# MLP down projection in a post-normalised decoder layer: seven 2x2-block products in two sweeps in place of eight blocks

## The chip, the cores and the metric

The kernel runs on one core of a Trainium2 chip. The metric is device time in microseconds (us) of one execution, lower is better.

## What is computed

One layer of a hybrid decoder: 512 tokens, width 1024, hidden width 4096, float32. Three sub-layers (a token mixer, cross-attention into 256 memory tokens, an MLP), each followed by `h = LayerNorm(ALPHA * h + f(h))`. The change concerns the third:

```
def sq_relu_mlp(h, w_up, b_up, w_down, b_down):
    u = jax.nn.relu(h @ w_up + b_up)
    return (u * u) @ w_down + b_down        # (512, 4096) @ (4096, 1024)

h = layer_norm(ALPHA * h + sq_relu_mlp(...), ln_ffn_g, ln_ffn_b)
```

## The kernel before

Every large product is done in three terms. An operand is split into a high part, the value cast to float32r, and a low part, the rest (`split`: a cast, then a subtraction); `mm3` adds high x high, high x low and low x high in PSUM. A matmul takes a 128 x 128 stationary tile and up to 512 moving columns.

The kernel's operations are recorded first and then put in order by a planner (`Program.issue`), which keeps a model of the engines, gives every operation a time, and issues in that order; operations recorded by `either` (as `any_tt`) go to the engine that the model finds free first. After that each engine's order is fixed, SyncE's list of DMAs too. All instructions are issued from line 355 of the kernel before, so the profile tells them apart by tile names. Tiles come from pools that are reused in turn: 4 buffers for raw weights (`wr`), 5 each for high and low parts of weights (`wh`, `wl`), 31 pages of 4 KB per partition, 8 PSUM banks.

The MLP works on blocks of 128 hidden units, 32 of them. `up(f)` loads a column block of `w_up` (`r_up`, 512 KB), splits it (`h_up`, `l_up`), runs 24 matmuls into a bank (`ps_up`), then relu on ScalarE (`ur`), the square on VectorE, and the split of the result into a page `u`. It does 16 blocks, then their part of the down projection: for each half of the 1024 columns, 4 banks (one for each block of 128 tokens, `ps_dn`) take 16 hidden blocks; VectorE adds them to the residual `res`. Then 16 more blocks, and the second part of the down projection in `gemm_tok`: eight banks (4 token blocks x 2 halves), the last four hidden blocks done token block by token block (`tail`), so that the norm of one token block (`after_ffn`) runs beside the matmuls of the next. For the last token block the second half goes in two quarters (`ps_dn2e`). The weights are `r_dn`, `h_dn`, `l_dn`. In the norm of the first three token blocks ScalarE scales and GpSimd adds the shift; the last is done on VectorE, and stored in halves.

Of the kernel before, what the change touches and what calls it, by code (L numbers as in the profile page):

```python
# [141 lines left out]
class Program:  # L142
# [97 lines left out]
    def issue(self, look):  # L240
# [28 lines left out]
        dma = 0.0  # L269
        holding, done = set(), [False] * len(ops)  # L270
        front = 0
        order = []

        def slots(op, at):

# [83 lines left out]
def f32(ap):  # L359
    return ap.bitcast(F32)  # L360
# [3 lines left out]
def trunk_kernel(ctx: ExitStack, tc: tile.TileContext, x, mem, ln_in_g, ln_in_b, w_in, gate_w2,  # L364
# [728 lines left out]

    def residual(res, t, parts, name):

        n = 512 if len(parts) == 2 else 256
        st = small.tile([128, D // n, 6], F32, "st_" + name)
        for cc, o in parts:
            nc.vector.tensor_tensor(res[t][:, cc], o, res[t][:, cc], op=OP.add)
            for c0 in range(cc.start, cc.stop, n):  # L1100
                nc.vector.bn_stats(st[:, c0 // n, :], res[t][:, c0:c0 + n])
        return mean_scale(st, name)
# [85 lines left out]
        gain_shift(res, gb, t, GAIN_LATER)  # L1188


    NF = DFF // 128 // 2
    slack[0] = M_SLACK

    def up(f, split):
# [4 lines left out]
        nc.scalar.activation(r, ps, AF.Relu, bias=bup[:, f:f + 1])  # L1199
        u = page([2, T], F32R, "u2")  # L1200
        nc.vector.tensor_tensor(r, r, r, op=OP.mult)
        nc.scalar.copy(u[:, 0, :], r)
        nc.vector.tensor_tensor(u[:, 1, :], r, f32(u[:, 0, :]), op=OP.subtract)
        return u

    us = [up(f, f < 4) for f in range(NF)]
    for c in range(2):
        banks = [bank("ps_dn") for _ in range(NT)]
        cc = slice(512 * c, 512 * c + 512)
        for f in range(0, NF, 2):  # L1210
            wh, wl = load_rows(w_down, 128 * f, "dn", 2, 512 * c, 512)
            for k in range(2):
                for t in range(NT):
                    tt = slice(128 * t, 128 * t + 128)
                    u = us[f + k]
                    mm3(banks[t], u[:, 0, tt], u[:, 1, tt], wh[:, k, :], wl[:, k, :], f + k == 0, f + k == NF - 1)
        for t in range(NT):
            nc.vector.tensor_tensor(res[t][:, cc], banks[t], res[t][:, cc], op=OP.add)
    us = [up(NF + f, False) for f in range(NF)]
    gbf = gb_rows(ln_ffn_g, ln_ffn_b, 1.0, "ffn")  # L1220

    def after_ffn(t, parts):
        y = res[t]
        mv, rs = residual(res, t, parts, "ffn")
        if t < NT - 1:
            nc.vector.scalar_tensor_tensor(y, y, mv[:, 0:1], gbf[0], op0=OP.subtract, op1=OP.mult)
            nc.scalar.activation(y, y, AF.Copy, scale=rs)
            pool_tt(y, y, gbf[1], OP.add)
            nc.sync.dma_start(out[128 * t:128 * t + 128, :], y)
            return  # L1230
        for cc in (slice(0, 512), slice(512, D)):
            nc.vector.scalar_tensor_tensor(y[:, cc], y[:, cc], mv[:, 0:1], gbf[0][:, cc], op0=OP.subtract, op1=OP.mult)
        for cc in (slice(0, 512), slice(512, D)):
# [43 lines left out]
```

## Time and profile before

| what | us |
|---|---|
| median of 3 runs (lowest, highest) | 845.61 (843.9, 846.23) |
| profiled execution, device time | 845.03 |
| profiled execution, first to last instruction (span) | 843.3 |
| TensorE busy | 815.2 |
| VectorE busy | 535.7 |
| ScalarE busy | 281.8 |
| GpSimd busy | 167.1 |

Busy times of different engines overlap. PE is TensorE's matmuls and PEld its weight loads, which run beside them; DVE is VectorE, ACT ScalarE, POOL GpSimd, SP SyncE, which issues the DMAs. The granted clock is a share of 2.4 GHz. All rows are of one profiled execution.

### The profile page before, as it was taken

What the parts mean: (1) busy time and instruction counts of PE and PEld (TensorE: products, weight loads), DVE (VectorE), ACT (ScalarE), POOL (GpSimd) and SP (SyncE); (2) the same over time, 40 slices, a digit from 0 to 9 for tenths busy, and PEclk for the clock granted to TensorE, in tenths of its full rate; (3) what the DMA queues carried; (4) which work ended last, traced back from release to release, by engine and by line L of the source; (5) the groups of instructions that cost most, each with busy time, mean ns of one, the idle gap of its engine ahead of it and who ended that gap; (6) DMA issues with size and microseconds to landing.
All of it is one profiled execution on the core that took longest, in us unless ns stands there. A gap on an engine that the chain in (4) does not pass through costs nothing.

```text
span 843.3 us, 11052 instructions
## 1 busy us (share of the span) xinstructions
PE 815.2 (97%) x4270; PEld 682.8 (81%) x4270; DVE 535.7 (64%) x936; ACT 281.8 (33%) x566; POOL 167.1 (20%) x179
## 2 busy tenths in 40 slices
PE   6999999999999899989999999999999999999996
PEld 4998768778777888888788898888888888888885
DVE  7657999997449984896544885444343444443337
ACT  4316633577445440334330344442000244430001
POOL 5300241465622210244420300000000000000005
PEclk8999999999999999999999999999999999999998
DMA  8440331603245444033313034333243333232102
GB/s 192 106 123 13 100 89 26 175 8 100 75 165 175 136 132 143 1 101 101 124 51 100 2 100 135 93 97 117 89 145 99 96 89 96 94 121 87 67 1 99
DMA packets 104660, 81.50 MB, mean 97 GB/s; under 512 B 21792, under 2 KB 90400, under 8 KB 104608
## 3 DMA queue, kind: packets, MB, share of 16 engines
q1 hardware_dynamic: 101296, 73.81, 29.6%
q10 hardware_dynamic: 3312, 7.00, 2.4%
q8 instruction: 33, 0.54, 0.3%
q14 instruction: 19, 0.16, 0.1%
HBM read 77.91 MB, written 2.10 MB: 95 GB/s over the span
## 4 chain that ended last, share of the span: by engine, by line
PE 75%; DVE 19%; issue 3%; ACT 1%; DMA 1%; POOL 1%; DVEq 0%; ACTq 0%; POOLq 0%
PE ps_up L355 21%; PE ps_dn L355 20%; PE ps_wmo L355 4%; PE ps_wo L355 4%; PE ps_q L355 3%; DVE acc L355 3%; PE ps_gv_iw L355 2%; PE ps_iq L355 2%; PE ps_km L355 2%; PE ps_z L355 2%; DVE res L355 2%; DVE m L355 2%; PE ps_vm L355 1%; PE ps_dq L355 1%; PE ps_mo L355 1%
## 5 line engine op out<-in xcount | busy, mean ns | idle before, releaser
L355 PE MATMUL ps_up<-h2T,h_up 128*128 128x512 f32 (+1 forms) x576 | 162.6, 368 | 0.0
L355 PE MATMUL ps_dn<-h_dn,u 128*128 128x512 f32 x504 | 155.4, 389 | 0.0
L355 PEld LDWEIGHTS ps_up<-h2T,h_up 128*128 128x128 f32 x576 | 105.2, 191 | 17.7 <-DVE h2T L355 0.2
L355 PEld LDWEIGHTS ps_dn<-h_dn,u 128*128 128x128 f32 x504 | 94.6, 188 | 19.6
L355 PE MATMUL ps_up<-h2T,l_up 128*128 128x512 f32 (+1 forms) x288 | 105.5, 368 | 0.5 <-DVE ve_mem L355 0.5
L355 PE MATMUL ps_dn<-l_dn,u 128*128 128x512 f32 x252 | 98.0, 389 | 0.0
L355 POOL TENSOR_TENSOR rs_ffn<-ve_ffn,mhalf 128x1 f32<-128x1 f32 x4 | 5.6, 1389 | 326.4 <-DVE ve_ffn L355 326.4
L355 PEld LDWEIGHTS ps_up<-h2T,l_up 128*128 128x128 f32 x288 | 54.8, 191 | 9.5 <-DVE l_up L355 0.7
L355 DVE TENSOR_SCALAR h_dn<-r_dn 128x1024 fp32r<-128x1024 f32 x21 | 14.6, 694 | 68.2 <-PE ps_dn L355 68.2
L355 DVE TENSOR_TENSOR ur<-ur 128x512 f32<-128x512 f32 x32 | 22.0, 691 | 55.0 <-ACT ur L355 55.0
L355 PEld LDWEIGHTS ps_dn<-l_dn,u 128*128 128x128 f32 x252 | 47.3, 188 | 9.9
L355 ACT ACTIVATE ur<-ps_up,bup 128x512 f32<-128x512 f32 x32 | 22.1, 690 | 73.0 <-PE ps_up L355 73.0
L355 PE MATMUL ps_q<-h1T,h_wmq 128*128 128x256 f32 (+1 forms) x192 | 45.2, 326 | 0.0
L355 ACT CAST h_up<-r_up 128x1024 fp32r<-128x1024 f32 x27 | 28.0, 1047 | 45.3 <-PE ps_dn L355 42.4
L355 DVE TENSOR_TENSOR l_up<-r_up,h_up 128x1024 fp32r<-128x1024 f32 x32 | 39.0, 1223 | 5.5 <-ACT h_up L355 5.3
L355 DVE TENSOR_TENSOR l_dn<-r_dn,h_dn 128x1024 fp32r<-128x1024 f32 x32 | 39.2, 1226 | 3.8 <-ACT h_dn L355 3.0
L355 PE MATMUL ps_wmo<-h_wmo,oT 128*128 128x512 f32 x128 | 40.7, 393 | 0.0
L355 PE MATMUL ps_wo<-h_wo,mix 128*128 128x512 f32 x128 | 40.3, 392 | 0.0
L355 DVE TENSOR_TENSOR u<-ur,u 128x512 fp32r<-128x512 f32 x32 | 22.1, 692 | 19.9 <-ACT u L355 19.9
L355 PEld LDWEIGHTS ps_q<-h1T,h_wmq 128*128 128x128 f32 x192 | 32.6, 195 | 2.5 <-DVE h1T L355 0.2
L355 PE MATMUL ps_q<-h1T,l_wmq 128*128 128x256 f32 (+1 forms) x96 | 31.1, 328 | 0.0
L355 ACT ACTIVATE res<-res,rs_ffn 128x1024 f32<-128x1024 f32 x3 | 3.5, 1152 | 79.8 <-POOL rs_ffn L355 79.8
(371 smaller groups left out, 1787.8 us busy)
## 6 DMA issues: line engine op xcount, KB each, us to landing
r_up<-in_w_up_dram SPq DMA_DIRECT2D x32, 512.0 KB, 3.8
r_dn<-in_w_down_dram SPq DMA_DIRECT2D x32, 512.0 KB, 3.7
r_kvv<-in_w_mem_kv_dram SPq DMA_DIRECT2D x8, 512.0 KB, 3.9
r_kvk<-in_w_mem_kv_dram SPq DMA_DIRECT2D x8, 512.0 KB, 4.0
r_wo<-in_w_out_dram SPq DMA_DIRECT2D x8, 512.0 KB, 4.7
r_wmq<-in_w_mem_q_dram SPq DMA_DIRECT2D x8, 512.0 KB, 4.2
r_wmo<-in_w_mem_o_dram SPq DMA_DIRECT2D x8, 512.0 KB, 3.3
x<-in_x_dram SPq DMA_DIRECT2D x8, 256.0 KB, 4.3
```

The source lines that it names most:

```text
L355: f(*[real(a) for a in args], **{k: real(a) for k, a in kwargs.items()})
```

## The change

The 2x2-block product of the squared activations by `w_down` (two token halves x two hidden blocks, by two hidden blocks x two column halves) is done with seven block products instead of eight (Strassen's algorithm, in Winograd's form). Two neighbouring hidden blocks make a pair, 16 pairs. The seven products are accumulated over all pairs, and only at the end put together. There are not enough banks for all of them, so there are two sweeps.

In the first sweep each pair runs its two up blocks and, behind those of the next pair, the products 1, 6 and 4, for two token blocks each (six banks beside the two of `ps_up`). The squared activations stay in a page `keep`; their sums and differences (`s2`, and others in place) are made on it, and operands are split as `ends` and `mid`. Of the weights, `r_dn0` and `r_dn1` are loaded, four differences are made (`t3`, and three in place), two of these are stored in a DRAM scratch (`t13`, one for each pair, two DMAs of 256 KB), and two groups are split (`h_dn512`, `h_dn1024`). Between the sweeps the six banks are worked into the residual. In the second sweep each pair splits its `keep` page (`a0`, `a1`), loads the scratch and the second weight block (512 KB each), splits both, and runs the products 7, 5, 3 and 2 in eight banks. The last `TAIL` = 4 pairs are split into pages (`b0`, `b1`) and run product by product, with the norms between them; all of the norm is now on VectorE. The square of `up` may go to VectorE or ScalarE; here it is always ScalarE, and it writes the page without a split.

```diff
-    us = [up(f, f < 4) for f in range(NF)]
-    for c in range(2):
-        banks = [bank("ps_dn") for _ in range(NT)]
...
-    gemm_tok(us, w_down, NF, NF, "dn2", after_ffn, ends=res[NT - 1])
+    def first_weights(i):
+        r0, r1 = raw_down(i, 0), raw_down(i, 1)
+        t3 = temp("t3")
+        any_tt(t3, r1[:, R], r0[:, R], OP.subtract)
+        any_tt(r0[:, R], r0[:, R], r0[:, L], OP.subtract)
+        kept = dram.tile([128, 1024], F32, f"t13_{i}")
+        nc.sync.dma_start(kept[:, L], r0[:, R])
+        nc.sync.dma_start(kept[:, R], t3)
+        sums.append(kept)
+        any_tt(r1[:, R], r1[:, R], r0[:, R], OP.subtract)
+        any_tt(r1[:, L], r1[:, R], r1[:, L], OP.subtract)
...
+        split_weights(r0[:, L], hi[0], lo[0])
+        split_weights(r1, hi[1], lo[1])
...
+    def first_products(i):
+        pg = keep[i]
+        block = lambda n: pg[:, n, :]
+        ends = page([2, 2, 256], F32R, "ends")
+        two_parts(ends[:, 0], ends[:, 1], pg[:, 0:4:3, :])
+        any_tt(block(0), block(0), block(1), OP.subtract)
+        any_tt(block(1), block(1), block(3), OP.add)
+        s2 = temp("s2", 256)
+        any_tt(s2, block(3), block(0), OP.subtract)
+        mid = temp("mid", 512, F32R).reshape(2, 256)
+        two_parts(mid[:, 0], mid[:, 1], s2)
+        any_tt(block(3), block(2), s2, OP.subtract)
+        b11, t2, t4 = first_weights(i)
...
+    for p in range(2):
+        six = temp("six")
+        nc.scalar.copy(six, banks["6", p])
+        add(p + 2, L, banks["4", p], OP.subtract)
+        add(p, L, banks["1", p])
+        nc.vector.tensor_tensor(six, banks["1", p], six, op=OP.add)
+        later.append(six)
...
+            for t, cc in ((p, R), (p + 2, L), (p + 2, R)):
+                any_tt(res[t][:, cc], res[t][:, cc], later[p], OP.add)
...
+    for p in range(2):
+        for n, name in enumerate(("7", "5", "3", "2")):
+            for i, todo in enumerate(rest):
+                products(banks, [todo[n]], p, False, i == TAIL - 1)
+            if name == "7":
+                add(p + 2, L, banks[name, p])
+                add(p + 2, R, banks[name, p])
+            elif name == "5":
+                add(p + 2, R, banks[name, p])
+                add(p, R, banks[name, p])
+                after_ffn(p + 2)
+            elif name == "3":
+                add(p, R, banks[name, p])
+            else:
+                add(p, L, banks[name, p])
+                after_ffn(p)
```

How the orders move is shown at three places. The first is SyncE's list of DMAs in the first sweep. Before, in the second group of up blocks and into the down projection, it holds loads only (a name in brackets is the engine or DMA queue whose semaphore the DMA waits for):

```order
L355 DMA r_up<-in_w_up_dram 128x8x128 [waits DMAHW2_49,DVE_49]
L355 DMA r_up<-in_w_up_dram 128x8x128 [waits DMAHW3_49,DVE_49]
L355 DMA r_up<-in_w_up_dram 128x8x128 [waits DMAHW4_49,DVE_49]
L355 DMA r_up<-in_w_up_dram 128x8x128 [waits DMAHW5_49,DVE_49]
L355 DMA r_up<-in_w_up_dram 128x8x128 [waits DMAHW6_49,DVE_49]
L355 DMA r_dn<-in_w_down_dram 128x2x512 [waits DMAHW7_49,DVE_49]
```

Now a round of the first sweep holds the two loads of `w_down`, the two stores into the scratch (`t_5`), each behind VectorE, and then the loads of the next up blocks:

```order
L356 DMA r_dn_5659<-in_w_down_dram 128x1024 [waits DMAHW2_49,DVE_49]
L356 DMA r_dn_5661<-in_w_down_dram 128x1024 [waits DMAHW0_49,DVE_49]
L356 DMA t_5_5666<-t_5663 128x512 [waits DVE_49]
L356 DMA t_5_5666<-r_dn_5659 128x512 [waits DMAHW5_49,DVE_49]
L356 DMA r_up<-in_w_up_dram 128x8x128 [waits DMAHW3_49,DMAHW1_49,Activation_49]
L356 DMA r_up<-in_w_up_dram 128x8x128 [waits DMAHW4_49]
```

The stores stand ahead of the loads of `w_up`, and SyncE takes its list in order.

The second place is TensorE where the last up block ends. Before, the down matmuls of that half follow at once, on pages made long before:

```order
L355 MATMUL ps_up<-h2T_4804,h_up 128x512 x2
L355 MATMUL ps_up<-h2T_4804,l_up 128x512
L355 MATMUL ps_dn_6695<-h_dn_6567,u_6152 128x512
L355 MATMUL ps_dn_6695<-l_dn_6573,u_6152 128x512
L355 MATMUL ps_dn_6695<-h_dn_6567,u_6152 128x512
L355 MATMUL ps_dn_6701<-h_dn_6567,u_6152 128x512
```

Now, behind the last up block and the first fifteen product matmuls of pair 14, TensorE has the last three of pair 14 (bank 5208 is product 4, second token block), three of product 7 of the second sweep (bank 6894), and pair 15, whose operands come from that last up block (5171 and 5196 are product 1, 5188 is product 4):

```order
L356 MATMUL ps_dn_5208<-h_dn_6751,ends 128x512
L356 MATMUL ps_dn_5208<-l_dn_6757,ends 128x512
L356 MATMUL ps_dn_5208<-h_dn_6751,ends 128x512
L356 MATMUL ps_dn_6894<-h_dn,a_6271 128x512
L356 MATMUL ps_dn_6894<-l_dn,a_6271 128x512
L356 MATMUL ps_dn_6894<-h_dn,a_6805 128x512
L356 MATMUL ps_dn_5171<-h_dn_6764,ends 128x512
L356 MATMUL ps_dn_5171<-l_dn_6769,ends 128x512
L356 MATMUL ps_dn_5188<-h_dn_6813,ends 128x512
L356 MATMUL ps_dn_5188<-l_dn_6815,ends 128x512
L356 MATMUL ps_dn_5196<-h_dn_6764,ends 128x512
L356 MATMUL ps_dn_5196<-l_dn_6769,ends 128x512
```

Of pair 15 the matmuls on the high part of `ends` come first, and the first matmuls of the second sweep have moved in between.

The third place is VectorE's end. Before, its last rows are the last token block (`res_2606`) alone, in two quarters at the end:

```order
L355 TENSOR_TENSOR res_2606<-ps_dn_6731,res_2606 128x512 [waits PE_49]
L355 BN_STATS st_ffn<-res_2606 128x6 [waits DVE_49]
L355 BN_STATS st_ffn<-res_2606 128x6
L355 TENSOR_TENSOR res_2606<-ps_dn2e,res_2606 128x256 [waits PE_49]
L355 BN_STATS st_ffn<-res_2606 128x6 [waits DVE_49]
L355 TENSOR_TENSOR res_2606<-ps_dn2e,res_2606 128x256 [waits PE_49]
L355 BN_STATS st_ffn<-res_2606 128x6 [waits DVE_49]
L355 BN_AGGR mv_ffn<-st_ffn 128x2 [waits DVE_49]
L355 TENSOR_SCALAR ve_ffn<-mv_ffn 128x1 [waits DVE_49]
L355 SCALAR_TENSOR_TENSOR res_2606<-res_2606,mv_ffn,gbc_ffn 128x512 x2
L355 SCALAR_TENSOR_TENSOR res_2606<-res_2606,rs_ffn,bbc_ffn 128x512 [waits DVE_49,Pool_49]
L355 SCALAR_TENSOR_TENSOR res_2606<-res_2606,rs_ffn,bbc_ffn 128x512 [waits DVE_49]
```

Now there are two token blocks in work at the end (`res_2608` and `res_2596`), in halves of 512, and the last sums from PSUM (bank 6982 is product 2) stand between the steps of the other block's norm:

```order
L356 TENSOR_SCALAR ve_ffn<-mv_ffn 128x1 [waits DVE_49]
L356 SCALAR_TENSOR_TENSOR res_2608<-res_2608,mv_ffn,gbc_ffn 128x512
L356 TENSOR_TENSOR res_2596<-res_2596,ps_dn_6982 128x512 [waits PE_49]
L356 SCALAR_TENSOR_TENSOR res_2608<-res_2608,mv_ffn,gbc_ffn 128x512
L356 SCALAR_TENSOR_TENSOR res_2608<-res_2608,rs_ffn,bbc_ffn 128x512 [waits DVE_49,Pool_49]
L356 SCALAR_TENSOR_TENSOR res_2608<-res_2608,rs_ffn,bbc_ffn 128x512 [waits DVE_49]
L356 BN_STATS st_ffn<-res_2596 128x6
L356 BN_AGGR mv_ffn<-st_ffn 128x2 [waits DVE_49]
L356 TENSOR_SCALAR ve_ffn<-mv_ffn 128x1 [waits DVE_49]
L356 SCALAR_TENSOR_TENSOR res_2596<-res_2596,mv_ffn,gbc_ffn 128x512 x2
L356 SCALAR_TENSOR_TENSOR res_2596<-res_2596,rs_ffn,bbc_ffn 128x512 [waits DVE_49,Pool_49]
L356 SCALAR_TENSOR_TENSOR res_2596<-res_2596,rs_ffn,bbc_ffn 128x512 [waits DVE_49]
```

Eight of these twelve are 512-wide steps, and the rows ahead of them are of the same kind.

## Rows read from the trace of the kernel before

**Rows 1.** The page, part 1: engine, busy us, share of the span, instructions.
```profile
PE 815.2 (97%) x4270; PEld 682.8 (81%) x4270; DVE 535.7 (64%) x936; ACT 281.8 (33%) x566; POOL 167.1 (20%) x179
```

**Rows 2.** The chain that ended last: start us, us, engine, work, count.
```profile
309.89 32.67 PE ps_wo L355 x144
...
493.99 80.91 PE ps_up L355 x416
574.89 87.04 PE ps_dn L355 x384
661.93 87.04 PE ps_up L355 x384
748.98 84.32 PE ps_dn L355 x372
833.29 2.88 PE ps_dn2e L355 x24
...
838.82 0.74 DVE res L355
839.56 0.66 DVEq L1273
```

**Rows 3.** Windows: us, length, busy of PE, PEld, DVE, ACT, POOL, clock, DMA, GB/s.
```profile
309.00:343.00 34.00, 34.00 (x157) 28.27 (x156) 17.78 (x22) 4.49 (x5) 0.56 (x1) 1.00 0.46 140
486.80:490.40 3.60, 3.59 (x17) 3.59 (x18) 3.60 (x5) 0.00 (x0) 1.47 (x1) 0.54 0.56 165
490.40:493.90 3.50, 3.50 (x30) 3.34 (x29) 1.26 (x4) 1.31 (x3) 0.00 (x0) 0.99 0.93 274
574.90:661.90 87.00, 87.00 (x385) 72.03 (x385) 35.42 (x39) 3.31 (x4) 0.00 (x0) 1.00 0.37 115
661.90:748.90 87.00, 87.00 (x386) 72.03 (x385) 41.15 (x48) 35.01 (x46) 0.00 (x0) 1.00 0.30 91
748.90:833.10 84.20, 84.20 (x373) 69.73 (x372) 36.67 (x47) 4.56 (x5) 8.39 (x5) 1.00 0.19 63
836.20:843.30 7.10, 0.00 (x0) 0.00 (x0) 3.92 (x8) 0.00 (x0) 2.45 (x2) 0.67 0.37 148
```

**Rows 4.** Groups by shape on VectorE: count, busy us, mean ns, idle before.
```profile
L355 DVE TENSOR_TENSOR l_dn<-r_dn,h_dn 128x1024 fp32r<-128x1024 f32 x32 | 39.2, 1226 | 3.8 <-ACT h_dn L355 3.0
...
L355 DVE TENSOR_TENSOR u<-ur,u 128x512 fp32r<-128x512 f32 x32 | 22.1, 692 | 19.9 <-ACT u L355 19.9
...
L355 DVE TENSOR_SCALAR h_dn<-r_dn 128x1024 fp32r<-128x1024 f32 x21 | 14.6, 694 | 68.2 <-PE ps_dn L355 68.2
...
L355 DVE TENSOR_TENSOR res<-ps_dn,res 128x512 f32<-128x512 f32 x16 | 11.0, 690 | 11.8 <-PE ps_dn L355 11.8
...
L355 DVE TENSOR_TENSOR mpT<-ps_mpt,mpT 128x256 fp32r<-128x256 f32 x16 | 6.1, 421 | 1.0 <-ACT mpT L355 0.9
...
L355 DVE BATCH_NORM_STATS2 st_ffn<-res 128x6 f32<-128x512 f32 x6 | 4.2, 695 | 0.2
...
L355 DVE TENSOR_SCALAR sp<-sa 128x512 fp32r<-128x512 f32 x6 | 2.5, 422 | 0.0
...
L355 DVE SCALAR_TENSOR_TENSOR res<-res,mv_ffn,gbc_ffn 128x512 f32<-128x512 f32 x2 | 1.4, 744 | 0.0
```

**Rows 5.** Groups by shape on ScalarE.
```profile
L355 ACT CAST h_up<-r_up 128x1024 fp32r<-128x1024 f32 x27 | 28.0, 1047 | 45.3 <-PE ps_dn L355 42.4 <-PE ps_wmo L355 2.9
L355 ACT ACTIVATE ur<-ps_up,bup 128x512 f32<-128x512 f32 x32 | 22.1, 690 | 73.0 <-PE ps_up L355 73.0
L355 ACT CAST u<-ur 128x512 fp32r<-128x512 f32 x32 | 19.8, 620 | 23.3 <-DVE ur L355 23.3
```

**Rows 6.** Groups by shape on GpSimd.
```profile
L355 POOL TENSOR_TENSOR res<-res,bbc_ffn 128x1024 f32<-128x1024 f32 x3 | 7.2, 2384 | 3.8 <-ACT res L355 3.8
```

**Rows 7.** The page, part 6: DMA issues, count, size, median us to landing.
```profile
r_dn<-in_w_down_dram SPq DMA_DIRECT2D x32, 512.0 KB, 3.7
```

More of the change, by code (lines that the diff above doesn't have):

```diff
@@ L246, in issue @@
                 ops[j].after.append(i)
+        self.order = order = []
         line = sorted(range(len(ops)), key=lambda i: ops[i].prio)
@@ L271, in issue @@
         front = 0
-        order = []
         def slots(op, at):
@@ L376, in pool @@
         got = ctx.enter_context(tc.tile_pool(name=name, bufs=bufs or 1, **kw))
-        return VPool(got, tag, bufs, space is not None)
+        return VPool(got, tag, bufs, space is PSUM)
     cst = pool("cst", None, 0)
@@ L1188, in trunk_kernel, with up @@
         gain_shift(res, gb, t, GAIN_LATER)
-    NF = DFF // 128 // 2
+    NP = DFF // 256
     slack[0] = M_SLACK
-    def up(f, split):
+    def up(f, split, to):
         wh, wl = load_cols(w_up, [(128 * f, 128, 0)], "up")
@@ L1219, in trunk_kernel @@
-    us = [up(NF + f, False) for f in range(NF)]
-    gbf = gb_rows(ln_ffn_g, ln_ffn_b, 1.0, "ffn")
-    def after_ffn(t, parts):
-        y = res[t]
[L1224 to L1231, printed above, removed]
+        b = bup[:, f:f + 1]
@@ new lines, in trunk_kernel, with products @@
+    sums = []
+    L, R = slice(0, 512), slice(512, 1024)
+    def products(banks, todo, p, start, stop):
+        tt = slice(128 * p, 128 * p + 128)
+        for name, (ah, al), (bh, bl) in todo:
+            mm3(banks[name, p], ah[:, tt], al[:, tt], bh, bl, start, stop)
+    def first_weights(i):
[9 more added lines that the diff above has]
+        any_tt(r1[:, L], r1[:, R], r1[:, L], OP.subtract)
+        hi = [wh_pool.tile([128, n], F32R, f"h_dn{n}") for n in (512, 1024)]
+        lo = [wl_pool.tile([128, n], F32R, f"l_dn{n}") for n in (512, 1024)]
+        split_weights(r0[:, L], hi[0], lo[0])
+        split_weights(r1, hi[1], lo[1])
+        return [(hi[0], lo[0]), (hi[1][:, R], lo[1][:, R]), (hi[1][:, L], lo[1][:, L])]
@@ new lines, in trunk_kernel @@
+    banks = {}
+    keep = []
+    def first_products(i):
[11 more added lines that the diff above has]
+        b11, t2, t4 = first_weights(i)
+        if i == 0:
+            for name in ("1", "6", "4"):
+                for p in range(2):
+                    banks[name, p] = bank(f"ps_dn{name}")
+        for p in range(2):
+            products(banks, [("1", (ends[:, 0, 0, :], ends[:, 1, 0, :]), b11), ("6", (mid[:, 0], mid[:, 1]), t2),
+                             ("4", (ends[:, 0, 1, :], ends[:, 1, 1, :]), t4)], p, i == 0, i == NP - 1)
@@ new lines, in add @@
+    def add(t, cc, o, op=OP.add):
+        nc.vector.tensor_tensor(res[t][:, cc], res[t][:, cc], o, op=op)
+    for i in range(NP):
+        pg = page([4, 256], F32, "keep")
+        keep.append(pg)
+        for e in range(2):
+            up(2 * i + e, i < 2, pg.reshape(1024)[:, 512 * e:512 * e + 512])
+        if i:
+            first_products(i - 1)
+    first_products(NP - 1)
+    later = []
+    for p in range(2):
+        six = temp("six")
[4 more added lines that the diff above has]
+        later.append(six)
@@ new lines, in trunk_kernel, with second_parts @@
+    nc.clock += DOWN_LATER
+    for p in range(2):
+        for t, cc in ((p, R), (p + 2, L), (p + 2, R)):
+            any_tt(res[t][:, cc], res[t][:, cc], later[p], OP.add)
+    nc.clock -= DOWN_LATER
+    gbf = gb_rows(ln_ffn_g, ln_ffn_b, 1.0, "ffn")
+    def second_parts(i, tail):
+        a = [page([4, 256], F32R, f"a{n}") for n in range(2)]
+        two_parts(a[0], a[1], keep[i])
+        r0 = wr_pool.tile([128, 1024], F32, "r_t13")
+        nc.sync.dma_start(r0, sums[i])
+        r1 = raw_down(i, 1)
+        right = []
+        for r in (r0, r1):
+            if tail:
+                hi, lo = (page([1024], F32R, f"b{n}") for n in range(2))
+            else:
+                hi, lo = wh_pool.tile([128, 1024], F32R, "h_dn"), wl_pool.tile([128, 1024], F32R, "l_dn")
+            two_parts(hi, lo, r)
+            right += [(hi[:, L], lo[:, L]), (hi[:, R], lo[:, R])]
+        left = [(a[0][:, n, :], a[1][:, n, :]) for n in range(4)]
+        return [("7", left[0], right[1]), ("5", left[1], right[0]), ("3", left[3], right[3]), ("2", left[2], right[2])]
@@ new lines, in trunk_kernel, with after_ffn @@
+    for i in range(NP - TAIL):
+        todo = second_parts(i, False)
+        if i == 0:
+            for name, *_ in todo:
+                for p in range(2):
+                    banks[name, p] = bank(f"ps_dn{name}")
+        for one in todo:
+            for p in range(2):
+                products(banks, [one], p, i == 0, False)
+    rest = [second_parts(i, True) for i in range(NP - TAIL, NP)]
+    def after_ffn(t):
+        y = res[t]
+        st = small.tile([128, 2, 6], F32, "st_ffn")
+        for c, cc in ((1, R), (0, L)):
+            nc.vector.bn_stats(st[:, c, :], y[:, cc])
+        mv, rs = mean_scale(st, "ffn")
+        for cc in (L, R):
```

33 lines of the change are left out of this document (16 added, 17 removed).

## The prediction

> **What bounds the kernel now.** The chain of waits comes first, read at its end [rows 2]: from 493.99 us to 836.17 us it holds nothing but TensorE, the up and down matmuls of the MLP one after the other, and only then VectorE for the last layer norm. The reader should see that no wait stands between the stretches: 384 down matmuls take 87.04 us, 384 up matmuls 87.04 us, which is 226.7 ns for each 512-column matmul whatever the tile. The windows say the same of the other engines [rows 3]: over 574.9 to 833.1 TensorE is busy all the time at granted clock 1.00 (2.4 GHz), VectorE 35 to 41 us of each stretch of 84 to 87, ScalarE 3 to 35, the DMA engines a share of 0.19 to 0.37. TensorE is busy 97% of the whole span [rows 1]. So in the MLP a matmul taken away is worth its 226.7 ns, as long as the engines with room left can do what replaces it. Ahead of the MLP the rows of every engine's order are the same in both kernels, so nothing moves before the first up blocks.
>
> **What it removes.** The down projection has 32 hidden blocks x 4 token blocks x 2 halves x 3 terms = 768 matmuls of 512 columns (384, 372, and 24 of half width in the last 2.88 us [rows 2]). Now it has 16 pairs x 7 products x 2 token blocks x 3 = 672, of the same shape. 96 x 0.2267 = 21.76 us; the 24 half matmuls took 2.88 us where twelve whole ones take 2.72, so 0.16 more. **Term 1: -21.92 us.** That the price stays 226.7 ns when accumulators change every three matmuls can be read: the mixer's output projection cycles eight banks like that, 144 matmuls in 32.67 us, 226.9 ns [rows 2], clock 1.00 [rows 3].
>
> **First sweep.** A pair is now 48 up matmuls and 18 products (1, 6, 4), 66 x 0.2267 = 14.96 us of TensorE. VectorE's share of a pair, counted in its order and priced by [rows 4]: three 1024-wide differences (3.68), two 1024-wide casts (1.39), one 512-wide cast (0.42), six 512-wide differences (4.15), five 256-wide sums (2.09): 11.7 us, 78%. ScalarE: one 1024-wide cast, two relus, two squares and two casts priced as the 512-wide one [rows 5]: 1.05 + 1.38 + 4 x 0.62 = 4.9 us. GpSimd has nothing. So no engine passes TensorE, if the in-order queues don't lock into each other. Two places were followed. The weight pools (5 buffers, filled in the order in which TensorE uses them) let the split of a block begin when the block five before it is used up, 9 us or more before TensorE wants it. And SyncE: the two stores of a pair wait for VectorE, and the next pair's two w_up loads stand behind them. The stores go out after VectorE's second instruction of the pair; load (3.7 us [rows 7]), cast and split (2.3 us) make 6 us from there, and TensorE wants the first of these blocks some 20 us after the stores. At the start, pair 0's products are wanted at 509.6 us (416 matmuls of the first stretch, of which the last twelve up blocks take 65.3 us, end at 574.9); VectorE, which has residual work left from the layer norm in both kernels, ends their splits at about the same time. **Term 2: 0**, and the cover is VectorE's 3.2 free us per pair; without it each us too long counts 14 times.
>
> **The joint of the sweeps.** Let T be the end of the last up matmul. TensorE's order puts 18 products of pair 14 and three of product 7 behind it, 21 matmuls, 4.76 us. In that time the last block goes through ScalarE: relu 0.69, a cast, square 0.62, two 1024-wide casts 2.1, cast 0.62, which gives pair 15's left operand at about T + 4.5 and its low part from VectorE at T + 6.1 (two 1024-wide differences stand ahead of it). TensorE does the six high matmuls first, until T + 6.1. Then the second sweep wants eight banks where the first holds six: product 5 may start when VectorE has subtracted product 4 from the residual, 3 when ScalarE has copied product 6, 2 when VectorE has added product 1 into it. Followed with [rows 4, 5] the last bank is free at about T + 12.9, and the 60th matmul behind T ends at T + 13.8 instead of 60 x 0.2267 = 13.6; the two 256-wide steps given to GpSimd (a quarter of its 2.38 us row [rows 6], 0.6 each) are the closest. I take **1 us for term 3**; below 0, above 4.7, the whole cover of 21 matmuls lost.
>
> **Second sweep.** A pair is 24 matmuls, 5.44 us. VectorE: three 1024-wide differences, 3.68 us; ScalarE three casts, 3.14 us [rows 4, 5]. VectorE comes late into it: behind the bank work it reaches the split of the third pair's first tile at T + 17 and ends it at T + 18.2, wanted at T + 19.7. From there it gains 1.8 us a pair. SyncE's loads are now two tiles of 512 KB per pair, 1.05 MB in 5.44 us = 193 GB/s. Over a whole stretch the trace has 115 GB/s at DMA share 0.37, and for 3.5 us 274 GB/s at 0.93 [rows 3]: 193 would be a share of 0.62 to 0.66. The last four pairs are held in pages so that TensorE can finish one accumulator after another; that wants the t13 tile of pair 15 about 14 us before its turn. By the load time of [rows 7] and four load buffers it is split some 2.6 us early. **Term 4: 0**, above 3.
>
> **The tail.** Let E be the end of the last matmul. Before, VectorE's last instruction ended at 840.22, 4.05 us after 836.17 [rows 2]. Now product 2 of token block 0 ends at E - 10.88 and VectorE reaches its addition at E - 10.5, with 7 additions from PSUM (4.83), 6 statistics (4.17) and 12 scale-and-shift steps (8.93) to do [rows 4], and six small ones that I put at 0.4 beyond what neighbours overlap: 18.3 us, so it ends at E + 7.8. It is VectorE that ends last now, since ScalarE and GpSimd, which took 1024-wide steps of the norm before, get none. **Term 5: +3.75 us**, below 0 (if waits were in the old tail that I have counted twice), above 6. The store after it is as long as before (the window from 836.2 [rows 3]).
>
> **Sum.** -21.92 + 0 + 1 + 0 + 3.75 = -17.2 us. The profiled execution took 845.03 us (span 843.3): 827.8. The median of the three runs is 845.61, 0.6 above it, so I write 828.4.
>
> [...] The row first: the clock falls to 0.54 over 486.8 to 490.4, after TensorE stood almost still for the layer norm, and there 256-column matmuls take 3.6 / 17 = 0.212 us [rows 3] instead of 2.88 / 24 = 0.120 [rows 2]. [...] The second sweep cycles eight banks. [...]
>
> **Rivals.** (a) The joint is worse: VectorE, with some 17 us of work between T and the third pair, falls behind by more than its 1.5 us, and TensorE waits for each split until VectorE has caught up. 4 to 10 us: 832 to 838. For it: the strict order puts six residual additions (4.1 us) ahead of that split. Against it: the lead regained later. (b) The other side: the stores at the head of SyncE's queue. If VectorE's round (11.7 us of work and its waits for ScalarE and TensorE) came to more than 14.96 us, stores, w_up loads and splits would all follow VectorE's pace, and every us beyond counts in 14 pairs. From 1.2 us beyond the gain is gone; at 2 us the time is 856. Against it: 3.2 us of room. For it: 17 instructions per pair, most of them with a wait. (c) The second sweep runs at the DMA rate. 16.8 MB in its 87 us need 193 GB/s; at 115, the highest that a long stretch shows, it would be 146 us, and the time 885. From about 160 GB/s downwards the gain is gone. Against it: 115 cost a share of only 0.37. (d) The change does not save what it says, since the clock falls in the second sweep: a 512-column matmul at the lower clock is about 0.40 us (0.2267 x 0.212 / 0.120), so the sweep's 87 us would be 153; a quarter of it at that clock adds 16.6 us and leaves 844. (e) Better: the additions of the tail and the joint are covered, 823 to 825.
>
> **How the numbers follow.** Forecast (825 to 832) 0.64; (a) 0.16; (b) 0.08; (c) 0.03; (d) 0.03; (e) 0.06. A measurement of this kernel can tell about 0.3%, 2.5 us, from no change. Faster is the forecast, (a), (e) and a little of (d): 0.87; same, within 843 to 848: 0.03; slower 0.10, from (b), (c) and half of (d). The range from 825 to 838 leaves out (b), (c), (d), most of (e) and the end of (a), 2 in 10.
>
> **What would show it.** In the new profile: 672 down matmuls of 128x512; TensorE without idle time from 494 us to about 815 except for about 1 us between 719 and 733, where the sweeps meet; granted clock 1.00 there; VectorE at about 0.75 to 0.8 in the first sweep; a DMA share near 0.6 in the second; 7 to 8 us from the last matmul to VectorE's last instruction. Wrong it would be if TensorE waits for a split or a bank in every pair (idle time that repeats each 15 or 5.4 us), if the clock falls after the joint, or if the loads of the second sweep take well over 4 us to land.

## The result and the profile after

| | before | changed |
|---|---|---|
| median, us | 845.92 | 832.26 |
| lowest to highest, us | 843.90 to 846.70 | 830.96 to 834.37 |
| profiled execution, us (span) | 845.03 (843.3) | 832.28 (830.6) |

The ratio is 0.9839, 95% interval 0.9821 to 0.9856: 13.7 us less, where the prediction had 17.2 less. A second measurement (below, on the chip of the first experiments) gave 0.9831, 0.9807 to 0.9856.

The page's first part, as in [rows 1]: 108 matmuls fewer: 96, and twelve more since the 24 half-width ones of before stood for twelve. VectorE has become busier by 95 us.

```profile
PE 795.8 (96%) x4162; PEld 665.3 (80%) x4162; DVE 630.6 (76%) x1108; ACT 326.7 (39%) x627; POOL 162.1 (20%) x179
```

The chain that ended last (start us, us, engine, work, count), to be held against [rows 2]. The first sweep stands there as a clock would: 18 down and 48 up matmuls by turns, every 14.96 us. Then the chain leaves TensorE for VectorE at 715.66 and returns at 725.78 only; from there 411 matmuls run without a wait.

```profile
510.92 4.11 PE ps_dn L356 x18
...
705.42 4.08 PE ps_dn L356 x18
709.50 6.13 PE ps_up L356 x27
715.66 1.23 DVE a L356
717.52 0.70 DVE r_dn L356
...
721.90 1.22 DVE a L356
724.33 0.98 issue
725.78 95.31 PE ps_dn L356 x411
821.71 2.07 DVE res L356 x3
824.82 0.72 DVE res L356 x2
826.06 0.74 DVE res L356
```

Let T be the end of the last up matmul and E the end of the last matmul, as in the prediction. The last up stretch begins at 709.50 and takes 10.88 us like those before it, so T is 720.38. E is 725.78 + 95.31 = 821.09. The 420 matmuls between them need 420 x 0.2267 = 95.2 us and took 100.7: **5.5 us are lost where the sweeps meet.** VectorE's last instruction ends at 826.06 + 1.41 = 827.47 (the row of 826.06 in VectorE's timeline is a pair of 1.41), which is E + 6.4; before it was 4.05 behind the last matmul.

The windows (start and end; length, busy time of PE, PEld, DVE, ACT and POOL with counts; clock; DMA share; GB/s) answer to [rows 3]. In the first sweep VectorE is busy 22.08 of 30 us; the second sweep loads at 189 to 262 GB/s, and TensorE does not stand still for it. In between, from 716 to 724, VectorE is full; from 720 to 728 TensorE has 2.27 and 2.96 of 4 us, and from 724 to 732 the clock is 0.82 and 0.75 in the mean. In windows of 0.5 us the clock is 1.00 up to 726.5, 0.50 in each from 727.0 to 730.0 and 1.00 from 730.5 on (0.60 and 0.99 in the two between), so these means stand for 0.50 from 726.6 to 730.0.

```profile
572.00:602.00 30.00, 30.00 (x134) 24.86 (x133) 22.08 (x34) 9.54 (x15) 0.00 (x0) 1.00 0.55 177
716.00:720.00 4.00, 4.00 (x20) 3.30 (x19) 3.86 (x6) 4.00 (x6) 0.00 (x0) 1.00 0.44 125
720.00:724.00 4.00, 2.27 (x9) 1.23 (x7) 3.93 (x7) 1.58 (x3) 0.00 (x0) 1.00 0.98 349
724.00:728.00 4.00, 2.96 (x9) 2.09 (x10) 3.06 (x5) 2.90 (x5) 0.00 (x0) 0.82 0.35 128
728.00:732.00 4.00, 4.00 (x15) 3.17 (x14) 2.90 (x5) 1.37 (x3) 0.86 (x2) 0.75 0.79 250
744.00:764.00 20.00, 20.00 (x90) 16.55 (x89) 17.36 (x16) 13.45 (x14) 0.00 (x0) 1.00 0.81 262
764.00:784.00 20.00, 20.00 (x90) 16.55 (x89) 16.38 (x15) 8.36 (x8) 0.00 (x0) 1.00 0.60 189
```

VectorE's timeline at this place (in brackets the idle time before and who ended it) shows what it was late with. For 4.17 us it stood in front of one instruction, the low part of pair 0's left operand (`a<-keep,a`, from `second_parts`). That wait ends with an up matmul, of which the instruction reads nothing: what it lacked was a page to write to, and the pages of the up matmuls' left operand (`h2T`) come free as the last up block ends. Behind it in VectorE's order stood pair 15's differences (`r_dn`), its cast and split, and then pair 14's `ends`, `keep`, `s`, `mid`, for which TensorE waited next. ScalarE's high part of pair 14's `ends` stands at 716.34 in its own order, so that VectorE's part could have run from 716.96 on; it began at 720.84.

```profile
710.81 0.69 DVE L356 TENSOR_TENSOR t<-r_dn,r_dn 128x512 f32<-128x512 f32 x1
715.66 1.23 DVE L356 TENSOR_TENSOR a<-keep,a 128x1024 fp32r<-128x1024 f32 x1 [4.17 <-PE ps_up L356]
716.80 0.68 DVE L356 TENSOR_TENSOR r_dn<-r_dn 128x512 f32<-128x512 f32 x1
...
718.98 0.69 DVE L356 TENSOR_SCALAR h_dn<-r_dn 128x1024 fp32r<-128x1024 f32 x1
719.70 1.23 DVE L356 TENSOR_TENSOR l_dn<-r_dn,h_dn 128x1024 fp32r<-128x1024 f32 x1
720.84 0.68 DVE L356 TENSOR_TENSOR ends<-keep,ends 128x512 fp32r<-128x512 f32 x1
721.56 0.42 DVE L356 TENSOR_TENSOR keep<-keep 128x256 f32<-128x256 f32 x1
721.90 1.22 DVE L356 TENSOR_TENSOR a<-keep,a 128x1024 fp32r<-128x1024 f32 x1
...
724.17 1.22 DVE L356 TENSOR_TENSOR a<-keep,a 128x1024 fp32r<-128x1024 f32 x1
725.31 0.42 DVE L356 TENSOR_TENSOR mid<-s,mid 128x256 fp32r<-128x256 f32 x1
```
```profile
716.34 0.62 ACT L356 CAST ends<-keep 128x512 fp32r<-128x512 f32 x1
```

TensorE's timeline of the same place: idle 0.75, 1.27 and 0.76 us, 2.8 together, for pair 14's `ends` and for both parts of its `mid`. Then the matmuls begin 0.42 or 0.43 us apart, eight of them from 726.59 to 729.98, where 0.2267 is usual.

```profile
721.59 0.73 PE L356 MATMUL ps_dn<-h_dn,ends 128*128 128x512 f32 x2 [0.75 <-DVE ends L356]
...
724.29 0.50 PE L356 MATMUL ps_dn<-h_dn,mid 128*128 128x512 f32 x1 [1.27 <-ACT mid L356]
...
725.78 0.51 PE L356 MATMUL ps_dn<-h_dn,mid 128*128 128x512 f32 x1 [0.76 <-DVE mid L356]
...
727.00 0.63 PE L356 MATMUL ps_dn<-l_dn,mid 128*128 128x512 f32 x1
727.42 0.63 PE L356 MATMUL ps_dn<-h_dn,mid 128*128 128x512 f32 x1
```

### The profile page after: what moved, and what is told of

It reads as the page before. It is cut to its first block, busy times and chain, and to the rows that moved or that the text cites. A ratio compares the mean times of both kernels' runs of the same rounds, so it can differ in the third digit from the quotient of the medians.

```text
span 830.6 us, 11271 instructions
## 1 busy us (share of the span) xinstructions
PE 795.8 (96%) x4162; PEld 665.3 (80%) x4162; DVE 630.6 (76%) x1108; ACT 326.7 (39%) x627; POOL 162.1 (20%) x179
## 4 chain that ended last, share of the span: by engine, by line
PE 73%; DVE 20%; issue 3%; ACT 2%; DMA 1%; POOL 1%; DVEq 0%; ACTq 0%; POOLq 0%
PE ps_up L356 20%; PE ps_dn L356 18%; PE ps_wmo L356 4%; PE ps_wo L356 4%; PE ps_q L356 4%; DVE acc L356 3%; PE ps_iq L356 2%; PE ps_gv_iw L356 2%; PE ps_km L356 2%; DVE res L356 2%; PE ps_z L356 2%; DVE m L356 2%; PE ps_vm L356 2%; PE ps_dq L356 1%; PE ps_mo L356 1%
## 5 line engine op out<-in xcount | busy, mean ns | idle before, releaser
L356 PE MATMUL ps_dn<-h_dn,a 128*128 128x512 f32 x192 | 59.9, 391 | 0.0
L356 DVE TENSOR_TENSOR l_dn<-r_dn,h_dn 128x1024 fp32r<-128x1024 f32 (+1 forms) x43 | 44.0, 1023 | 7.0 <-ACT h_dn L356 5.6
L356 PE MATMUL ps_dn<-h_dn,ends 128*128 128x512 f32 x128 | 47.4, 394 | 0.7 <-DVE ends L356 0.7
L356 PEld LDWEIGHTS ps_dn<-h_dn,a 128*128 128x128 f32 x192 | 36.3, 189 | 7.9 <-DVE six L356 0.3
L356 PE MATMUL ps_dn<-l_dn,a 128*128 128x512 f32 x96 | 37.6, 392 | 0.0
L356 ACT CAST h_up<-r_up 128x1024 fp32r<-128x1024 f32 x17 | 17.7, 1054 | 30.1 <-PE ps_dn L356 20.7
L356 PEld LDWEIGHTS ps_dn<-h_dn,ends 128*128 128x128 f32 x128 | 24.3, 190 | 6.2 <-DVE ends L356 1.2
L356 PEld LDWEIGHTS ps_wo<-h_wo,mix 128*128 128x128 f32 x128 | 24.0, 188 | 4.9
L356 PEld LDWEIGHTS ps_wmo<-h_wmo,oT 128*128 128x128 f32 x128 | 24.0, 188 | 4.8
L356 DVE TENSOR_SCALAR h_up<-r_up 128x1024 fp32r<-128x1024 f32 x15 | 10.4, 692 | 23.1 <-PE ps_up L356 19.6
```

The costliest lines, as they stand in the source:

```text
L356: f(*[real(a) for a in args], **{k: real(a) for k, a in kwargs.items()})
```

## The experiments

T to E and E to VectorE's last end are read from each kernel's profiled execution as above; the medians carry the noise of the part ahead of the MLP too (T lay between 717.6 and 720.9, but for 725.2 with seven more VectorE steps and 734.2 with one page more). A median of one run is to be taken with that noise in mind, and the two right-hand columns tell more.

| kernel | median, us (runs) | T to E | E to VectorE's end |
|---|---|---|---|
| changed, again | 831.17 (4) | 100.6 | 6.4 |
| splits later | 826.77 (4) | 96.9 | 6.4 |
| tail shared | 829.52 (4) | 101.4 | 4.65 |
| both | 825.80 (5), again 826.11 (4) | 96.9, 97.0 | 4.65 |
| both, no GpSimd at the joint | 824.20 (5) | 95.3 | 4.65 |
| one page more | 835.90 (6) | 95.45 | 6.4 |
| fewer products | 819.43 (1) | 87.85 | 8.7 |
| no stores | 831.64 (1) | 101.4 | 6.4 |
| 3 more VectorE steps per pair | 829.74 (1) | 97.7 | 6.4 |
| 7 more VectorE steps per pair | 841.92 (1) | 105.45 | 6.4 |
| more DMA | 826.67 (1) | 96.7 | 6.4 |

Theory: the 5.5 us come from one instruction that blocks an in-order queue. Rival: VectorE has more work at the joint than it can do there, in whatever order.

**The changed kernel again.** 

> The changed kernel once more, on the same chip as the three variants, so that they can be compared with it and not only with the kernel before. Every theory expects 832 us, 13 to 14 below the kernel before, with 5 to 6 us lost between the last up matmul and the steady second sweep.


Measured: 831.17 us, 0.9831 (0.9807 to 0.9856) of the kernel before. It is the neighbour for the next three, which ran on the same chip.

**The splits of the second sweep later.**
```diff
+        ahead, nc.ahead = nc.ahead, 100.0
         two_parts(a[0], a[1], keep[i])
+        nc.ahead = ahead
```


> The same work, but at the joint the splits of the left operands of the second sweep may enter an engine's order only 100 places ahead of their use, so that on VectorE the preparation of pair 15 and the steps of pair 14 stand ahead of them. Theory (VectorE's in-order queue is blocked for 4.17 us by one split that waits for a page): from the last up matmul to the last matmul takes about 96 to 97 us instead of 100.7, the clock does not drop there, and the time is 828 (827 to 829.5). Rival (VectorE simply has too much work at the joint, so its order does not matter): 831 to 833, and TensorE's waits of about 2.8 us come back at other places.


Measured: 826.77 us, ratio 0.9785 (0.9761 to 0.9809), 4.4 us below its neighbour. T to E is 96.9 us and the granted clock stays at 1.00. VectorE's timeline of this kernel: the work of pairs 14 and 15 stands ahead of the split, which waits for nothing. VectorE then waits 4.22 us for ScalarE (`r_t` is the load of the scratch); behind it stand second-sweep work and pair 15's steps on its last up block. That this wait costs nothing is shown further down: it is there too, 4.21 us, in the kernel without GpSimd at the joint, where TensorE waits for nothing.

```profile
709.66 0.42 DVE L356 TENSOR_TENSOR mid<-s,mid 128x256 fp32r<-128x256 f32 x1
...
710.33 0.69 DVE L356 TENSOR_TENSOR t<-r_dn,r_dn 128x512 f32<-128x512 f32 x1
...
713.30 0.69 DVE L356 TENSOR_SCALAR h_dn<-r_dn 128x1024 fp32r<-128x1024 f32 x1
714.10 1.23 DVE L356 TENSOR_TENSOR l_dn<-r_dn,h_dn 128x1024 fp32r<-128x1024 f32 x1
715.43 1.22 DVE L356 TENSOR_TENSOR a<-keep,a 128x1024 fp32r<-128x1024 f32 x1
720.87 1.23 DVE L356 TENSOR_TENSOR l_dn<-r_t,h_dn 128x1024 fp32r<-128x1024 f32 x1 [4.22 <-ACT h_dn L356]
```

The rival falls: the same work in another order costs 3.7 us less. But the edit moved more than one instruction: ScalarE's high part of pair 14's `ends` came earlier too, at 704.97, 13.6 us before T, and stood at 716.34, 4.0 before T, in the changed kernel. Which of the two mattered is told by the run with one page more. What is left, 1.7 us, comes back below.

**The tail shared again.**
```diff
+        if t != 1:
+            nc.vector.scalar_tensor_tensor(y, y, mv[:, 0:1], gbf[0], op0=OP.subtract, op1=OP.mult)
+            nc.scalar.activation(y, y, AF.Copy, scale=rs)
+            pool_tt(y, y, gbf[1], OP.add)
+            nc.sync.dma_start(out[128 * t:128 * t + 128, :], y)
+            return
```


> The last layer norm of the token blocks other than the last one goes back to 1024-wide steps, one on VectorE, the scale on ScalarE, the shift on GpSimd, as the kernel before had it; the last token block stays as it is. Theory (VectorE's amount of work sets the tail): VectorE's last instruction ends at 4.5 to 5.5 us after the last matmul instead of 6.4, so 831 us, 1 to 2 below the changed kernel. Rival (the handing over to ScalarE and GpSimd, about 1.15 and 2.4 us, ends as late): no difference, 832, with GpSimd's instruction the last one in the chain.


Measured: 829.52 us, ratio 0.9808 (0.9784 to 0.9831), 1.65 below its neighbour. VectorE's last instruction ends at E + 4.65 instead of 6.4, and it is still VectorE's that ends the chain, so the rival falls. The joint was as in the changed kernel, or a little worse (clock 0.79, 0.50 and 0.86 over 4 us each from 720 to 732; read as times at 0.50 and at 1.00, the three together are some 6.8 us at 0.50, against 3.4 in the changed kernel).

**Both.** 

> The later splits and the shared tail together. If both theories hold, the two gains add up, since they lie at different places: about 826.5 us (825.5 to 828.5). If only the one on the joint holds, 828; if only the one on the tail, 831; if neither, 832.


Measured: 825.80 us, ratio 0.9770 (0.9746 to 0.9794). Both gains add up: 3.7 in T to E and 1.75 behind E, and 5.4 us below the neighbour.

**Both, once more, and without GpSimd at the joint.** In the kernel with both changes TensorE still waited 1.3 us, for VectorE's `six`. VectorE's timeline there, and GpSimd's:

```profile
726.96 1.22 DVE L356 TENSOR_TENSOR l_dn<-r_dn,h_dn 128x1024 fp32r<-128x1024 f32 x1
728.09 3.43 DVE L356 TENSOR_TENSOR l_dn<-r_t,h_dn 128x1024 fp32r<-128x1024 f32 x1
731.45 1.27 DVE L356 TENSOR_TENSOR six<-ps_dn,six 128x512 f32<-128x512 f32 x2
```
```profile
727.97 2.48 POOL L356 TENSOR_TENSOR a<-keep,a 128x1024 fp32r<-128x1024 f32 x1 [2.42 <-ACT a L356]
```

A subtraction that takes 1.22 us in the row above it took 3.43 here. GpSimd's ran from 727.97 to 730.45; VectorE's ended at 731.52, 1.07 us behind that, as if it had begun only then. In the changed kernel too: there a subtraction of 2.44 us (734.67 to 737.11) ended 1.08 us behind one of GpSimd's (733.63 to 736.03). VectorE's residual additions, which read one operand from PSUM, kept their 0.6 to 0.7 us each there. It goes the other way too, in the run with one page more: there VectorE's split began first and took 1.22 us, and GpSimd's took 3.38, against 2.40 in the changed kernel, where it had begun first.
```profile
743.37 1.22 DVE L356 TENSOR_TENSOR l_dn<-r_t,h_dn 128x1024 fp32r<-128x1024 f32 x1
```
```profile
743.48 3.38 POOL L356 TENSOR_TENSOR l_dn<-r_dn,h_dn 128x1024 fp32r<-128x1024 f32 x1 [0.80 <-ACT h_dn L356]
```
```diff
     def any_tt(o, a, b, op):
+        if alone[0]:
+            nc.vector.tensor_tensor(o, a, b, op=op)
+            return
...
+    alone[0] = True
     first_products(NP - 1)
```


> The kernel with both changes once more, as the neighbour of the next one: about 825 to 826 us, 96.9 us from the last up matmul to the last matmul.

> The kernel with both changes, and from pair 15's preparation on no subtraction of two tiles in SBUF is given to GpSimd; VectorE does these (three at the joint: two 256-wide and one 1024-wide). Theory (a VectorE subtraction of two SBUF tiles stands still while GpSimd has such an instruction: 3.43 us instead of 1.23 beside GpSimd's 2.48 us, and TensorE waited 1.3 us for the step behind it): VectorE's split takes 1.23 us again, the 1.3 us wait goes or falls under 0.5, 95.5 to 96.3 us from the last up matmul to the last matmul, and the time is 0.7 to 1.3 us lower. Rival (VectorE has no room for the work that GpSimd did, 2.0 us at VectorE's durations): the wait stays at 1.3 us or grows, no difference or slower.


Measured: 826.11 us (ratio 0.9775, 0.9762 to 0.9788) and, without GpSimd, 824.20 (0.9758, 0.9745 to 0.9772). The chain of the second has no wait left where the sweeps meet, 420 matmuls in one row, at 0.2268 us each:

```profile
706.76 10.88 PE ps_up L356 x48
717.64 95.27 PE ps_dn L356 x420
```

VectorE now does GpSimd's 2 us as well and is done sooner (its additions of `six` end at T + 17.6 instead of T + 19.2). The ranges of the two medians overlap (824.99 to 827.24 and 822.57 to 826.72); T to E, 97.0 and 95.3, parts them. One thing more changed: `six` came to stand ahead of the split that had been held up. So the run does not separate the two by itself; by the rows of the kernel with both changes, without the 2.2 us of standing still `six` would have ended at about 729.9, before TensorE stopped at 730.9, in the old order as well (an estimate from these rows). This is the fastest of the versions that compute the whole product, 20.5 us below the kernel before by its ratio.

**One page more.** The page count goes from 31 to 32 and the temporaries from eight to six. The planner takes it from there.
```diff
-    half = pool("half", "t2", 8)
-    pages = pool("pages", "pg", 31)
+    half = pool("half", "t2", 6)
+    pages = pool("pages", "pg", 32)
```


> The changed kernel with 32 pages instead of 31 (and six 512-wide temporaries instead of eight, to make room for it). The planner, left as it is, now puts the low part of pair 0's left operand a whole round earlier in VectorE's order; the splits of pairs 1 to 3 stand where they then find pages only as the last up matmuls end, ahead of the last steps of pair 14. Theory (the 4.17 us wait on VectorE was for a page, and what stood behind it was late for that reason alone): the wait is gone, pair 15's differences run about 4 us earlier, and from the last up matmul to the last matmul it takes 96 to 99 us instead of 100.6; the time is 828 to 830.5. Rival (the wait was for something else, such as the bank or the high part): the 4 us wait stays in front of the same work and the time is 831 to 832.


Measured: 835.90 us, ratio 0.9886 (0.9861 to 0.9910). The forecast of the time was wrong, that of the joint was too modest: T to E is 95.45 us, all 420 matmuls in one row of the chain, without VectorE's wait. ScalarE's high part of pair 14's `ends` is as late as in the changed kernel (730.05, 4.1 us before T), but VectorE follows at once, 3.5 us before T instead of 0.5 behind it. VectorE's order from pair 15's differences to pair 14's `mid` is the same but for the places of the left operands' splits. So it was VectorE's wait that made the joint late, and not ScalarE's place. The time went up since everything ahead of the MLP was later: the first 18 down matmuls begin at 524.73 in the profiled execution (840.83 us, the longest of the six), against 510.92 in the changed kernel. What of the page or the temporaries did that was not taken apart.

```profile
524.73 4.11 PE ps_dn L356 x18
...
723.31 10.88 PE ps_up L356 x48
734.19 95.45 PE ps_dn L356 x420
```
```profile
730.05 0.61 ACT L356 CAST ends<-keep 128x512 fp32r<-128x512 f32 x1
```
```profile
730.69 0.69 DVE L356 TENSOR_TENSOR ends<-keep,ends 128x512 fp32r<-128x512 f32 x1
```

**Fewer products.**
```diff
         for one in todo:
+            if one[0] == "5" and i:
+                continue
```


> Leaves out product 5 of pairs 1 to 11 in the second sweep, so its output is not the reference's: 66 matmuls fewer, and the loads and splits of the pairs stay. Theory (TensorE alone sets the second sweep, term 1's price of 226.7 ns): 15.0 us less, about 816, and a pair of the second sweep takes 4.08 us. Rival (c), the second sweep is near the DMA rate: 1.05 MB in 4.08 us are 257 GB/s, and if that can't be had, TensorE waits for splits in every pair and the gain is under 10 us.


Measured: 819.43 us, about 12 below the changed kernel and not 15. T to E fell by 12.7 of the 15.0, and the tail grew by 2.3. With 4.08 us of TensorE per pair, VectorE is full and TensorE begins to miss its splits, though the loads come at 261 and 282 GB/s, more than the 193 that the full second sweep wants:

```profile
744.00:764.00 20.00, 19.80 (x88) 16.07 (x87) 17.16 (x16) 14.93 (x16) 0.00 (x0) 1.00 0.80 261
764.00:784.00 20.00, 19.11 (x85) 15.46 (x83) 19.69 (x18) 11.04 (x11) 0.00 (x0) 1.00 0.87 282
```

A pair came to 4.08 + 2.2 / 11 = 4.3 us in the mean, so in the full sweep, at 5.44, TensorE sets the pace with about 1 us per pair to spare, and rival (c) falls. What would set the pace at 4.3 us is open: the chain of this run goes through casts on ScalarE, splits on VectorE and three loads of 3.7 to 5.2 us.

**No stores.**
```diff
-        kept = dram.tile([128, 1024], F32, f"t13_{i}")
-        nc.sync.dma_start(kept[:, L], r0[:, R])
-        nc.sync.dma_start(kept[:, R], t3)
-        sums.append(kept)
...
-        nc.sync.dma_start(r0, sums[i])
+        nc.sync.dma_start(r0, w_down[256 * i:256 * i + 128, :])
```


> Leaves out the stores of the weight sums: the second sweep loads plain rows of the weights in their place, so its output is not the reference's; all work on the engines stays. Theory (the stores and their place at the head of the DMA queue cost nothing, term 2 is 0): 831, within 2 us, with the same period of 14.96 us in the first sweep. Rival (b), stores hold up the loads behind them: 5 us or more come back.


Measured: 831.64 us, period 14.96 us, T to E 101.4. The stores cost nothing that one run can show; T to E is 0.8 above the changed kernel's; the matmuls from 724.90 to 729.16 begin 0.42 or 0.43 us apart, as they do at clock 0.50 in the changed kernel.

**More work for VectorE.** (three or seven of these, ahead of the stores)
```diff
+        more = temp("more")
+        for _ in range(3):
+            nc.vector.tensor_tensor(more, r1[:, R], r1[:, L], op=OP.subtract)
```


> Adds three 512-wide subtractions, which nothing uses, to VectorE's work for each pair of the first sweep, ahead of the stores: 2.07 us per pair, inside the 3.2 us of room that the prediction gives as cover of term 2. Theory (the cover is there): 831 to 834, period of a pair still 14.96 us, VectorE some 0.92 busy in the first sweep. Rival (the in-order waits take up the room already): TensorE waits in every pair, and the time is 840 or more.

> Seven such subtractions per pair, 4.8 us, 1.6 us beyond the room. Theory (VectorE then sets the pace and SyncE's stores and loads follow it, the mechanism of rival (b)): a pair takes about 16.6 us, and the time is about 831 + 14 x 1.6 = 853, less where the early pairs are covered by buffers: 845 to 856. If the time stays under 838, the count of VectorE's work in a pair was too high; over 870, its waits come on top of its work.


Measured: 829.74 and 841.92 us. With three, every pair still takes 14.96 us, and VectorE is 0.84 busy (0.92 was expected). With seven, VectorE is busy 29.0 of 30 us and TensorE begins to wait for splits. The window of the same 30 us, with three and then with seven:

```profile
572.00:602.00 30.00, 30.00 (x134) 24.86 (x133) 25.23 (x41) 9.54 (x15) 0.00 (x0) 1.00 0.55 176
```
```profile
572.00:602.00 30.00, 29.83 (x131) 24.09 (x130) 29.02 (x47) 10.11 (x16) 0.00 (x0) 1.00 0.62 193
```

From the first down matmul to T it takes 213.9 us with seven (511.3 to 725.2) against 209.5, 4.4 us more, and T to E 105.45, 4.8 more. The 22 us of the sum did not come, since a subtraction added only (25.23 - 22.08) / 6 = 0.52 us of busy time, not 0.69: VectorE's instructions overlap with their neighbours. Seven add 3.7 us to 11.0 and just fit into 14.96. What a pace truly set by VectorE costs was therefore not reached. That three more made the joint better (97.7) is taken for the planner's order again: VectorE's wait for the split of pair 0 was 2.37 us there instead of 4.17, with the added steps ahead of it.

**More DMA.**
```diff
+        spare = dram.tile([128, 1024], F32, f"spare_{i}")
+        nc.sync.dma_start(spare, w_down[256 * i:256 * i + 128, :])
```


> The changed kernel, with a further copy of 512 KB from one place in DRAM to another per pair of the second sweep: 290 GB/s wanted instead of 193, and the copies stand in the same queue as the loads. Theory (term 4: the second sweep's loads have room, 193 GB/s was at a share of 0.54 to 0.60): a few us of waits at most where the joint has used up the lead, 831 to 838. Rival (c), the rate is the bound: 16.8 + 8.4 MB at about 262 GB/s, the most that 20 us of the changed kernel's trace show, take 96 us instead of 87, and if a copy counts twice (read and written), 128 us: 840 to 872.


Measured: 826.67 us, but it does not answer its question: nothing held the copies back, and the planner issued all sixteen from 628.4 to 708.3 us, in the first sweep. There the rate rose to 252 and 281 GB/s over 30 us each (630 to 690), and the pairs kept their 14.96 us. Again the order at the joint came out otherwise (T to E 96.7, VectorE's wait for the split 0.26 us).

## Why the prediction came out as it did

The direction and the size were right, at 3.5 us off; by the median the time lies where the forecast (825 to 832) and rival (a) (832 to 838) meet. In part that is luck: the joint cost 4.5 us more than the sum had, and the tail 1.45 less, which hides a third of it.

**Term 1, -21.92.** Right. The 66 matmuls of a pair take 14.96 us and, without waits, 420 matmuls take 95.27. That a pair of the second sweep is bound by TensorE is shown by the run with fewer products.

**Term 2, 0.** Right, shown by the period of 14.96 us in all the pairs, and by the runs without stores and with three more steps. VectorE's work in a pair was sized too high: 11.0 us (22.08 / 2.005 pairs) instead of 11.7, since summed durations count twice what neighbours overlap.

**Term 3, the joint, +1.** Too small: 5.5, beyond even the 4.7 that the prediction gave as its upper bound. The step that failed is the one that followed VectorE behind T "with [rows 4, 5]". It took VectorE's order there as a list of durations, with a wait for ScalarE and the banks, and spoke of pages for the last four pairs only. In the trace, the low part of pair 0's left operand could have its page only when an up matmul had read the last of a page's content, and 4.17 us went by with runnable work behind it. That the blocked place in the queue is the cause is shown from two sides: the later splits took 3.7 of the 5.5 us away, and with one page more the wait was gone and so was the loss (T to E 95.45), with ScalarE's order at this place unchanged. The second run had another plan ahead of the MLP and six temporaries, so it is clean for the joint only. The parts of the 5.5: 2.8 us of idle time in three waits; about 0.8 more since a first matmul behind a wait takes 0.11 longer (0.50 for 0.39) and loses the 0.16 by which it else overlaps the one before; 1.6 from the lower clock, since the eight matmuls from 726.59 to 729.98 take 0.424 us each instead of 0.2267; the last 0.3 is spread over the rest. Rival (a) had the size but not the place: it had the third pair's splits late, and behind 725.78 TensorE waited for none; pair 14's own steps were.

**Term 4, 0.** Right: 411 matmuls without a wait, at up to 262 GB/s over 20 us.

**Term 5, the tail, +3.75.** 2.3. The mechanism holds, VectorE ended last, and sharing the norm gave 1.7 back. The size was off for the reason of term 2: between E - 10.9 and E + 6.4 VectorE was busy 16.9 us where the sum had 18.3.

**Sum.** -21.9 + 5.5 + 2.3 = -14.1, and the MLP began later by 1.3 us in this execution than in the one before (the first down matmul at 510.92, expected at 509.6): -12.8, as the two profiled executions differ (845.03 to 832.28).

**Rival (d).** It did not come. The second sweep ran at clock 1.00 from 732 us on, cycling eight banks, and from 744 to 804 us TensorE was busy 60.00 of 60 us. Of the prediction's signs of being wrong one came, the clock: it fell once in the MLP, from 726.6 to 730.0 us, behind three waits and with TensorE busy 2.27 and 2.96 of 4 us. In the kernel without waits at the joint it did not fall. A matmul at that level took 0.424 us where the prediction's estimate was 0.40.

**A slip.** In rival (c) the time would be 887 us by its own figures (828 - 87 + 146), not 885; nothing else hangs on it.

## What to carry to other kernels

Where an engine works in order, ask of each early instruction what buffer it needs and when that comes free: work put there in advance may stand in front of work that is due, as VectorE's split of pair 0 did here for 4.17 us. Where the pattern of the matmuls changes within a kernel, as where the sweeps meet here (T to E 100.7 us, and 95.3 without a wait), follow the engines that prepare them across that place, with their waits and not only their durations. And here, with fewer matmuls, what VectorE took over showed in the joint (5.5 us) and the tail (2.3 us), not in the steady part.

## What the runs showed of the hardware

A VectorE subtraction with both inputs in SBUF took longer beside a GpSimd instruction of that kind: 3.43 us beside 2.48 of GpSimd (both changes), 2.44 beside the end of one of 2.40 (the changed kernel), 1.22 alone; and GpSimd's took 3.38 instead of 2.40 where VectorE's had begun first (one page more). In the first two, VectorE's ended 1.07 and 1.08 us behind GpSimd's, as if it had stood still until then; why, no run shows. Additions with one input from PSUM ran on: four in 2.48 us from 732.27 in the changed kernel, 0.62 each, with GpSimd busy from 733.63. The prediction priced GpSimd's steps at their own time (0.6 us) and not at VectorE's lost time, though the trace of the kernel before had such a place: a split of `l_wmo`, 128x1024, took 2.98 us (from 411.22) beside a GpSimd step of 2.40 (from 410.71), and ended 1.09 us behind it.

Two or three short waits of TensorE were followed by a lower granted clock (0.82 and 0.75 over 4 us each in the changed kernel; 0.50 over 4 us with the tail shared), and so was a single one of 4.2 us (with seven more VectorE steps: the matmul at 735.26, 0.8 us behind that wait, took 0.63 us, as at 0.50 in the changed kernel, and the clock was 0.76 over the 10 us from 730 and 0.90 over the next ten). A single one of 1.3 us was not (1.00 with both changes), nor one of 2.1 us (1.00 with three more VectorE steps).

Of the 2.4 GHz that stand with the granted clock ahead of the result, the runs show this much. At 1.00 a 512-column matmul took 0.2267 us and a 256-column one 0.120, so 256 columns 0.107. At 0.50 they took 0.427 (the changed kernel, starts from 727.00 to 729.56) and 0.213 (the kernel before, from 487.42 to 489.98), so 256 columns 0.213. That is 2.4 and 1.2 columns per ns, an estimate from these four times.
